# A longer list of steps at two seams of a two-layer trunk, its loads held back, and an attention mask written by VectorE

## The chip, the core and the metric

The kernel runs on one core of one Trainium2 chip. The core has a TensorE (matrix products, PE in the profile, its weight loads apart as PEld), a VectorE (DVE), a ScalarE (ACT), a GpSimd (POOL, all but unused here) and a SyncE (SP), whose queue issues most of the loads. The engines run side by side and wait for each other on semaphores. The metric is the device time of one execution in microseconds, the median of several runs.

## The reference

A trunk of two layers over a sequence of 1024 rows of 1024 columns, in float32:

```
for l in (0, 1):
    h = modulate(rmsnorm(x, norm_g[l, 0]), sh_m, sc_m)
    if l == 0: y = short_conv_mixer(h, ...)              # 1024 -> 3072, gated conv, -> 1024
    else:
        k_nope, v, k_pe = shared_kv(x, ...)              # latent keys and values of 8 heads
        y = mla_mixer(h, ..., k_nope, v, k_pe, ...)      # attention, blocks of 128 queries
    x = x + g_m * rmsnorm(y, norm_g[l, 1])
    h = modulate(rmsnorm(x, norm_g[l, 2]), sh_f, sc_f)
    y = square(relu(h @ w_up)) @ w_down                  # 1024 -> 4096 -> 1024
    x = x + g_f * rmsnorm(y, norm_g[l, 3])
```

In the attention a block of 128 queries sees the keys up to its own end, and a mask in chunks of 64 applies:

```
s = q_nope . k_nope + q_pe . k_pe
mask = (k // 64) <= (q // 64)
s = where(mask, s, finfo(float32).min);  p = softmax(s);  o = p @ v
```

Within the last 128 columns of a block's scores it is one quadrant that the mask blanks: the first 64 queries against the last 64 keys.

## The kernel before

**Products.** A float32 factor is kept as two parts: a rounded high part, written by a ScalarE copy (L176), and the low rest, written by a VectorE subtraction (L177). A product is three matmuls (`mm`, L173): low by high, high by low, high by high. Most of TensorE's work has this form and this line.

**The up projections.** `w_up` has 32 blocks of 128 columns, taken as 16 pairs. After a first, pre-split part, a pair is computed by a scheme with seven half-size products (Strassen's kind): sums of the pair's four quarters are formed by VectorE (`pair_sums`, L529, L530, L534, L537) and split into t2, s2 and t3; the products 5, 4 (from t2), 6 (from s2), 7 and 3 (from t3) follow, and VectorE adds them up (the takes at L583, L594, L603, L609). Loads of a pair are `load_pair`; the raw weights go into a ring of four buffers, or, for each third pair, into two buffers of their own (`up`, tag `raw`).

**The seams.** Ahead of each of the two MLPs, the stage before ends in rows of the residual stream: eight steps of norms and sums, each row then transposed (`tr0_0` and so on, L421), scaled by ScalarE (`tu`, L425) and split by VectorE into the moving factors (`b0`, L432, L433), and quarters summed (`D1` to `D9`, `P1` to `P5`, L445, L455, L458). `first_pairs` mixes this with the first up products: `fi` and `se` are the first and second products of the first five blocks, `ev1` and `ev2` their evictions, `spa` and `spd` the splits of the fourth and fifth block's weights (each loaded by `late` into one buffer `w`), `S1`, `t2a`, `t2d`, `S2`, `s2a`, `S3`, `s2d`, `t3a`, `t3d` the sums and splits of the first pair (a: high part by ScalarE, d: low part by VectorE) and `p3_0` to `p7_3` the products of the first pair, each in four parts. The order of these steps stands in the list `ORDER`. While the list runs, `pinned` fixes that order on every engine but SyncE. The scheduler of the framework orders the rest by its own priorities. When the list is done, six VectorE sums add up the first pair (L737 to L742), and the second pair is loaded, summed and split by `all_pairs`, as the later ones are. The two seams lie at about 374 to 441 us and 1512 to 1580 us.

**SyncE's queue.** Loads are issued in the queue's order; a load whose buffer isn't free holds up those behind it. The loads of the fourth block's weight and of the first pair are written outside `pinned`; the scheduler has put them in the midst of the stage before (the output product of the first layer's mixer, whose factors are the loads `raw<-hd` and conv_out_w).

**The attention.** `scores` computes a block of 128 queries of one head against n keys into PSUM (`big`) with five matmuls for each 512 columns (L1437), then a further matmul adds the mask: `mask_l` is 1 in the first 64 columns of one row, `mask_r` is -2^127, and the product lands on the last 64 columns (L1438). VectorE takes the negative maximum of each row (L1440), ScalarE writes the exponential and its sum (L1443), VectorE scales by the reciprocal (L1447, L1448), and TensorE transposes the result (L1463) for the product with the values. There are 8 heads of 8 blocks: 64 such calls.

Of the kernel before, what the change touches and what calls it, by code (L numbers as in the profile page):

```python
# [8 lines left out]
F32 = mybir.dt.float32  # L9
F32R = mybir.dt.float32r  # L10
# [34 lines left out]
mm5 tr0_0 tr0_1 tu0_0 mm6 add5 b0_0 sq5 rc4 pre4 stt5 tu0_1 xad5 tr0_2 tr0_3 tu0_2 add6 mm7 sqx5 b0_2 sq6 b0_1 rc5  # L45
pre5 stt6 tu0_3 xad6 dma5 tr0_4 tr0_5 tu0_4 add7 sqx6 tr0_6 b0_3 tu0_6 mul7 fi0 tu0_5 rc6 sq7 b0_4 b0_5 pre6 tr0_7
fi1 stt7 ev1_0 tu0_7 b0_6 sqx7 b0_7 fi2 ev1_1 rc7 S1 dma7 pre7 dma6 tr1_0 ev1_2 se0 tu1_0 P1_0 D1_0 D3_0 P2_0 tr1_1
D2_0 ev2_0 spa3 se2 D6_0 D4_0 P3_0 spd3 P4_0 tu1_1 D5_0 fi3 D8_0 P5_0 D7_0 ev2_2 D9_0 P1_1 t2a D3_1 tr1_2 D1_1 ev1_3
se1 t2d P2_1 tu1_2 D6_1 S2 P1_2 D2_1 se3 s2a D3_2 spa4 D4_1 ev2_1 spd4 P3_1 P4_1 D7_1 fi4 ev2_3 s2d D5_1 D8_1 P5_1
S3 p4_0 D9_1 t3a p6_0 D1_2 tr1_3 t3d P2_2 p6_1 tu1_3 D2_2 p5_1 D6_2 p7_0 P3_2 D4_2 p3_0 P1_3 D7_2 ev1_4 p7_1 P4_2  # L50
D5_2 se4 D3_3 P5_2 D8_2 D9_2 D1_3 p4_2 ev2_4 D2_3 p3_2 P2_3 D4_3 P3_3 p5_2 D6_3 P4_3 p7_2 D5_3 p6_2 D8_3 P5_3 p5_0
D7_3 p3_1 D9_3 p4_1 p4_3 p5_3 p7_3 p3_3 p6_3
# [4 lines left out]
C_ID, C_ML, C_MR, C_T = 0, 128, 256, 320  # L57
C_COLS = 2368
# [3 lines left out]
def trunk_kernel(ctx: ExitStack, tc: tile.TileContext, x, c, ada_w, ada_b, norm_g, conv_in_w, conv_w,  # L62
# [104 lines left out]

    mask_l = cp.tile([P, P], F32R, name="mask_l")
    mask_r = cp.tile([P, CHUNK], F32R, name="mask_r")
# [380 lines left out]
    def all_pairs(up, ops, jobs):  # L550
# [6 lines left out]
        for raws, begun, quarter, done, between in jobs:  # L557
            ra, rb = raws()
# [3 lines left out]
            if begun is None:  # L562
                w = up_split(up, ra)
# [10 lines left out]
            for part in pair_sums(up, ra, rb):  # L574
                rest.update(part or {})
# [70 lines left out]
    def first_pairs(seam, acts, up, wmat, ws, ops):  # L646
# [48 lines left out]
        late(3)  # L695
        a, b = load_pair(wmat, 0, up)
        a11, a12, a21, a22 = a[:, 0:4, :], a[:, 4:8, :], b[:, 0:4, :], b[:, 4:8, :]
        sums = {}
# [4 lines left out]
        def begin():  # L703
# [3 lines left out]
        def s2():  # L707
            sums["s2"] = high(a21, tuple(up.tile([P, 4, P], F32R, tag="s2" + "hl"[i], name=nm("s2"), bufs=1) for i in range(2)))

        acts["S1"] = begin  # L710
        acts["t2a"] = lambda: sums.update(t2=high(b))
        acts["t2d"] = lambda: low(sums["t2"], b)
        acts["S2"] = lambda: diff(a21, a22, a11)
        acts["s2a"] = s2
        acts["S3"] = lambda: diff(a12, a12, a21)
        acts["s2d"] = lambda: low(sums["s2"], a21)
        acts["t3a"] = lambda: sums.update(t3=high(a))
        acts["t3d"] = lambda: low(sums["t3"], a)

        def piece(j, kk):  # L720
# [4 lines left out]
            w = sums[w]  # L725
# [5 lines left out]

        with pinned():
            for name in ORDER:
                acts[name]()
            p1, cb = ca[0][:, HALF:], row_tile()
            c21, c22 = halves(cb)
            nc.vector.tensor_tensor(c21, p1, out_[6], op=ALU.add)  # L737
            nc.vector.tensor_tensor(c22, c21, out_[5], op=ALU.add)
            nc.vector.tensor_tensor(c21, c21, out_[4], op=ALU.add)
            nc.vector.tensor_tensor(p1, c22, out_[3], op=ALU.add)  # L740
            nc.vector.tensor_tensor(c22, c22, out_[7], op=ALU.add)
# [902 lines left out]
```

## Time and profile before

| what | value |
|---|---|
| median of 3 runs | 2173.43 us (2172.13 to 2174.46) |
| the profiled execution | 2171.63 us |
| its span, first to last instruction | 2169.8 us |
| its mean granted TensorE clock | 0.992 |
| busy: TensorE, VectorE, ScalarE | 2098.7, 1524.6, 1061.4 us |
| list of steps of the first seam | 372 to 436 us |
| list of steps of the second seam | ends at 1575.7 us |
| scores and products of the attention | 1135 to 1430 us |

A row of a timeline shows the start and the duration in us, the engine, the line, the operation, out<-in, the form and the count; in brackets what the engine waited for just before, and for how long. Names are those of the program without their numbers: `one`, `mm`, `tp` and `big` are PSUM banks, `slot` and `ring` are split factors, `uphi` and `uplo` are the high and low parts of t2 or t3 (or of a block's weight), `s` is s2 (its two parts, numbers and suffixes left out), `q` and `sums` the sums of quarters, `y` rows of results. VectorE and ScalarE rows are longer than their spacing by some 0.1 us, since an instruction starts before the one ahead has written its end.

### The profile page before, as it was taken

The numbers are of one execution on the slowest core, as the hardware profiler recorded it, in microseconds if no ns is written. First come the engines' busy times: TensorE is split into PE (matmuls) and PEld (weight loads), VectorE is DVE, ScalarE is ACT, GpSimd is POOL, SyncE is SP. The second block draws the span as 40 slices with busy tenths as digits, with TensorE's granted clock in tenths as the row PEclk, the third lists the DMA queues.
The fourth block names the chain that finished last, engine by engine and source line by source line (L and its number), as shares of the span: only waits on it lengthen the run. The fifth ranks groups of instructions, "written<-read, shape, count | busy, mean of one in ns | idle before, by whom it ended". The sixth has DMA issues, their size and how long they took to land.

```text
span 2169.8 us, 25308 instructions
## 1 busy us (share of the span) xinstructions
PE 2098.7 (97%) x9702; PEld 1729.0 (80%) x9702; DVE 1524.6 (70%) x2001; ACT 1061.4 (49%) x1512; POOL 4.0 (0%) x8
## 2 busy tenths in 40 slices
PE   6999999999999999999899999999999999999998
PEld 5888878778888778888777888877778887788887
DVE  5877766977665578956788776665976665558556
ACT  4533354845444434344665555564844544444342
POOL 0000000000000000000000000000000000000000
PEclk9999999999999999999999999999999999999999
DMA  8344464356543976445224231053355553853243
GB/s 244 103 148 132 145 219 140 89 187 204 167 150 112 328 267 243 167 144 175 78 61 120 76 113 45 25 175 131 89 184 174 174 176 112 305 194 127 97 146 136
DMA packets 242335, 330.95 MB, mean 153 GB/s; under 512 B 18629, under 2 KB 143906, under 8 KB 242214
## 3 DMA queue, kind: packets, MB, share of 16 engines
q1 hardware_dynamic: 204328, 248.57, 36.2%
q10 hardware_dynamic: 37886, 80.77, 9.8%
q8 instruction: 76, 1.25, 0.2%
q14 instruction: 45, 0.37, 0.0%
HBM read 248.55 MB, written 80.74 MB: 152 GB/s over the span
## 4 chain that ended last, share of the span: by engine, by line
PE 72%; DVE 13%; ACT 7%; DMA 6%; issue 2%; ACTq 0%; SPq 0%; DVEq 0%
PE one L173 36%; PE mm L173 18%; PE tp L173 7%; PE big L173 5%; DMA raw<-in_ada_w_dram 3%; PE big L1437 2%; ACT junk L258 2%; DVE y L318 1%; DVE raw L319 1%; DVE acc L198 1%; PE tp L1463 1%; DMA raw<-in_mlp_up_w_dram 1%; DVE y L312 1%; DMA raw<-ha 1%; DVE small L1440 1%
## 5 line engine op out<-in xcount | busy, mean ns | idle before, releaser
L173 PE MATMUL one<-slot,uphi 128*128 128x512 f32 x1240 | 382.1, 390 | 0.0
L173 PEld LDWEIGHTS one<-slot,uphi 128*128 128x128 f32 x1240 | 232.8, 188 | 48.7 <-issue 0.5
L173 PE MATMUL big<-slot 128*128 128x512 f32 x1152 | 266.9, 392 | 2.4 <-ACT y L887 1.9
L173 PEld LDWEIGHTS big<-slot 128*128 128x128 f32 x1152 | 216.2, 188 | 47.9 <-ACT y L887 2.4
L173 PE MATMUL one<-slot,uplo 128*128 128x512 f32 x620 | 242.8, 392 | 2.1 <-ACT y L581 2.1
L173 PE MATMUL one<-ring,ring 128*128 128x512 f32 x1008 | 232.4, 391 | 6.9 <-DVE ring L177 6.9
L176 ACT ACTIVATE ring<-w 128x1024 fp32r<-128x1024 f32 x98 | 103.7, 1058 | 261.5 <-PE tp L173 131.2
L173 PEld LDWEIGHTS one<-ring,ring 128*128 128x128 f32 x1008 | 188.2, 188 | 49.9 <-DVE ring L177 5.7
L177 DVE TENSOR_TENSOR uplo<-raw,uphi 128x1024 fp32r<-128x1024 f32 x121 | 147.7, 1223 | 78.0 <-ACT uphi L176 78.0
L177 DVE TENSOR_TENSOR ring<-w,ring 128x1024 fp32r<-128x1024 f32 x98 | 119.8, 1223 | 110.4 <-ACT ring L176 110.4
L176 ACT ACTIVATE uphi<-raw 128x1024 fp32r<-128x1024 f32 x121 | 128.0, 1059 | 136.8 <-PE one L173 82.4
L173 PE MATMUL mm<-ring,ring 128*128 128x512 f32 x672 | 162.5, 390 | 0.0
L173 PE MATMUL tp<-ring,ring 128*128 128x512 f32 x672 | 161.8, 389 | 0.0
L173 PE MATMUL mm<-slot,uphi 128*128 128x512 f32 x504 | 159.1, 397 | 0.0
L173 PEld LDWEIGHTS mm<-ring,ring 128*128 128x128 f32 x672 | 125.7, 188 | 27.1 <-DVE ring L177 0.6
L173 PEld LDWEIGHTS tp<-ring,ring 128*128 128x128 f32 x672 | 126.2, 188 | 26.2
L198 DVE SCALAR_TENSOR_TENSOR acc<-raw,csil,acc 128x1024 f32<-128x1024 f32 x88 | 112.8, 1282 | 46.6 <-DMA raw<-in_ada_w_dram 43.7
L173 PEld LDWEIGHTS one<-slot,uplo 128*128 128x128 f32 x620 | 116.4, 188 | 27.8 <-ACT y L581 3.3
L177 DVE TENSOR_TENSOR ring<-raw,ring 128x1024 fp32r<-128x1024 f32 x98 | 119.5, 1220 | 18.1 <-ACT ring L176 18.1
L173 PE MATMUL one<-slot,s 128*128 128x512 f32 x468 | 117.4, 402 | 9.2 <-DVE s L177 9.2
L173 PEld LDWEIGHTS one<-slot,s 128*128 128x128 f32 x468 | 91.0, 195 | 29.4 <-DVE s L177 10.1
L173 PEld LDWEIGHTS mm<-slot,uphi 128*128 128x128 f32 x504 | 95.6, 190 | 20.4 <-issue 1.4
(278 smaller groups left out, 3449.5 us busy)
## 6 DMA issues: line engine op xcount, KB each, us to landing
ha<-y ACTq DMA_DIRECT2D x196, 256.0 KB, 2.9
raw<-ha SPq DMA_DIRECT2D x98, 512.0 KB, 4.3
raw<-in_ada_w_dram SPq DMA_DIRECT2D x80, 512.0 KB, 4.7
raw<-in_mlp_up_w_dram SPq DMA_DIRECT2D x70, 512.0 KB, 5.1
w<-in_mlp_down_w_dram SPq DMA_DIRECT2D x56, 512.0 KB, 4.9
raw<-hd SPq DMA_DIRECT2D x24, 512.0 KB, 4.9
xs<-raw ACTq DMA_DIRECT2D x24, 512.0 KB, 2.8
raw<-xs SPq DMA_DIRECT2D x24, 512.0 KB, 3.8
```

What stands on the lines that cost most here:

```text
L173: nc.tensor.matmul(out_, lhs[a], rhs[b], start=first and i == 0, stop=last and i == 2, skip_group_check=more)
L176: nc.scalar.activation(hi, src, AF.Copy)
L177: nc.vector.tensor_tensor(lo, src, hi.bitcast(F32), op=ALU.subtract)
L198: nc.vector.scalar_tensor_tensor(acc, raw, s, acc, op0=ALU.mult, op1=ALU.add)
L258: nc.scalar.activation(junk, src, AF.Square, accum_out=ss)
L312: nc.vector.tensor_tensor(y, y, p_, op=ALU.add)
L318: nc.vector.scalar_tensor_tensor(y, y, rroot(ss), self.gmb, op0=ALU.mult, op1=ALU.mult)
L319: nc.vector.tensor_tensor(xr, xr, y, op=ALU.add)
L1437: nc.tensor.matmul(o_, a, m_, start=j == 0, stop=j == 4 and b * HALF + w < n)
L1440: nc.vector.tensor_reduce(mx, sp[:, :n], AX.X, ALU.max, negate=True)
L1463: nc.tensor.transpose(p_[:, c:c + P], pts[4 * hf + i][:, j * P:(j + 1) * P], ident)
```

## The change

Three things change.

**The list.** `ORDER` goes on through the second pair: `nS1`, `nt2a`, `nt2d`, `nS2`, `ns2a`, `nS3`, `ns2d`, `nt3a`, `nt3d` are its sums and splits, and `o6`, `o5`, `o4`, `o3`, `o7` are the six sums of the first pair, which stood behind the list. All steps have another order. `all_pairs` takes the second pair as it comes out of the list (`ready`).

**The loads.** The loads of the second pair (now in the two buffers of `up`, i % 3 == 1), of the fourth block's weight and of the first pair are written, in this order, under `pinned` for SyncE alone, so each stands behind the one before it, and behind the last load of x.

**The mask.** The mask matmul and its factors go (with 192 columns of the constants' input; the first load of constants has 128 columns instead of 320). VectorE writes -2^127 into the 64 by 64 quadrant of PSUM before the maximum.

SyncE around the first seam: `w` is the fourth (then the fifth) block's weight, names with in_mlp_up_w are weights of the up projection, those with hd and conv_out_w factors of the stage before, those with in_x rows of x. Before:

```order
L127 DMA raw_397_2470<-in_conv_out_w_dram 128x1024
L127 DMA w_478_2881<-in_mlp_up_w_dram 128x8x128
L127 DMA raw_398_2474<-hd2_118 128x1024
L127 DMA raw_399_2478<-in_conv_out_w_dram 128x1024
L127 DMA raw_400_2482<-hd3_119 128x1024
L127 DMA raw_479_2883<-in_mlp_up_w_dram 128x8x128
L127 DMA raw_480_2885<-in_mlp_up_w_dram 128x8x128
L127 DMA raw_409_2598<-in_conv_out_w_dram 128x1024
L127 DMA raw_410_2602<-hd4_120 128x1024
```

And after, further on in the same queue:

```order
L127 DMA raw_477_2875<-in_x_dram 128x1024
L127 DMA raw_478_2877<-in_mlp_up_w_dram 128x8x128
L127 DMA raw_479_2879<-in_mlp_up_w_dram 128x8x128
L127 DMA w_480_2881<-in_mlp_up_w_dram 128x8x128
L127 DMA raw_481_2883<-in_mlp_up_w_dram 128x8x128
L127 DMA raw_482_2885<-in_mlp_up_w_dram 128x8x128
L127 DMA w_533_3169<-in_mlp_up_w_dram 128x8x128
```

The weight (478, now 480), the first pair (479 and 480, now 481 and 482) moved behind the last load of x (477), with the second pair (478 and 479) ahead of them.

VectorE at the end of the first seam's list. Before, `q_563` is D9_3, 565 and 566 are the second pair's raw blocks, 569 and 573 the low parts of its t2 and t3, 571 that of its s2, 576 and 577 the third pair's blocks:

```order
L458 TENSOR_TENSOR q_563_3409<-sums_562_3383,q_563_3409 128x512
L177 TENSOR_TENSOR uplo_569_3458<-raw_566_3452,uphi_568_3457 128x1024
L530 TENSOR_TENSOR raw_588_3608<-raw_588_3608 128x512
L534 TENSOR_TENSOR raw_566_3452<-raw_566_3452,raw_565_3450 128x512
L537 TENSOR_TENSOR raw_565_3450<-raw_565_3450,raw_566_3452 128x512
L529 TENSOR_TENSOR raw_576_3512<-raw_576_3512,raw_577_3514 128x512
L737 TENSOR_TENSOR y_564_3437<-y_519_3104,mm_552_3317 128x512
L177 TENSOR_TENSOR uplo_573_3468<-raw_565_3450,uphi_572_3467 128x1024
L738 TENSOR_TENSOR y_564_3437<-y_564_3437,mm_557_3342 128x512
L177 TENSOR_TENSOR s2_571_3463<-raw_566_3452,s2_570_3462 128x512
```

After, with the second pair in 478 and 479, its low parts 555 (t2), 572 (t3) and 569 (s2):

```order
L681 TENSOR_TENSOR uplo_555_3326<-raw_479_2879,uphi_554_3325 128x1024
L455 TENSOR_TENSOR q_567_3415<-sums_564_3380,q_567_3415 128x512
L702 TENSOR_TENSOR raw_479_2879<-raw_479_2879,raw_478_2877 128x512
L526 TENSOR_TENSOR raw_576_3508<-raw_576_3508,raw_577_3510 128x512
L702 TENSOR_TENSOR raw_478_2877<-raw_478_2877,raw_479_2879 128x512
L757 TENSOR_TENSOR y_570_3439<-y_531_3151,mm_563_3370 128x512
L681 TENSOR_TENSOR s2_569_3437<-raw_479_2879,s2_568_3436 128x512
L681 TENSOR_TENSOR uplo_572_3445<-raw_478_2877,uphi_571_3444 128x1024
L757 TENSOR_TENSOR y_570_3439<-y_570_3439,mm_556_3328 128x512
```

The low part of s2 now stands ahead of that of t3 and of the sum with product 5, and the fourth pair's sums (raw_587, raw_588) have left the list.

TensorE at the border of the second and third pair. Before, `one_567` is the second pair's running bank, `one_578` the third pair's; slot_368 with s2 is product 6, slot_371 product 5, slot_370 product 3:

```order
L173 MATMUL one_567_3454<-slot_371_2322,uplo_569_3458 128x512
L173 MATMUL one_567_3454<-slot_371_2322,uphi_568_3457 128x512 x2
L173 MATMUL one_578_3516<-slot_368_2319,s2_582_3525 128x512
L173 MATMUL one_578_3516<-slot_368_2319,s2_581_3524 128x512 x2
L173 MATMUL one_578_3516<-slot_368_2319,s2_582_3525 128x512
```

After (the second pair's bank is `one_573`):

```order
L170 MATMUL one_573_3466<-slot_371_2318,uplo_555_3326 128x512
L170 MATMUL one_573_3466<-slot_371_2318,uphi_554_3325 128x512 x2
L170 MATMUL one_573_3466<-slot_370_2317,uplo_572_3445 128x512
L170 MATMUL one_573_3466<-slot_370_2317,uphi_571_3444 128x512 x2
L170 MATMUL one_578_3512<-slot_368_2315,s2_582_3521 128x512
```

The first three matmuls of the second pair's product 3 moved ahead of the third pair's product 6. On VectorE the take of the bank before them (L583) and the low part of the third pair's s2 have changed places: before the split stood first, now the take does.

The diff, without most of the list's rows:

```diff
-mm5 tr0_0 tr0_1 tu0_0 mm6 add5 b0_0 sq5 rc4 pre4 stt5 tu0_1 xad5 tr0_2 tr0_3 tu0_2 add6 mm7 sqx5 b0_2 sq6 b0_1 rc5
...
-D7_3 p3_1 D9_3 p4_1 p4_3 p5_3 p7_3 p3_3 p6_3
+mm5 tr0_0 tr0_1 add5 tu0_0 mm6 b0_0 sq5 rc4 tu0_1 stt5 pre4 b0_1 tr0_2 tr0_3 add6 tu0_2 mm7 tu0_3 xad5 sq6 b0_3 sqx5
+stt6 dma5 rc5 xad6 pre5 tr0_4 add7 tr0_5 sqx6 b0_2 tu0_4 rc6 sq7 fi1 mul7 b0_4 tu0_5 dma6 stt7 pre6 tr0_6 tr0_7 fi2
+tu0_6 b0_5 sqx7 b0_6 tu0_7 rc7 fi0 pre7 b0_7 ev1_2 nS1 ev1_1 spa3 S1 tr1_0 ev1_0 se2 tu1_0 spd3 P1_0 D1_0 dma7 D3_0
...
+P5_3 p6_0 nt2d p4_1 p3_2 D9_3 nS2 p6_3 nS3 p7_3 ns2a o6 p4_3 nt3a ns2d p5_3 nt3d o5 o4 p3_3 o3 o7
@@ load_pair
-            raw = up.tile([P, D], F32, tag="raw", name=nm("raw"), bufs=2) if up and i % 3 == 0 else raw_tile()
+            raw = up.tile([P, D], F32, tag="raw", name=nm("raw"), bufs=2) if up and i % 3 == 1 else raw_tile()
@@ all_pairs
-            for part in pair_sums(up, ra, rb):
-                rest.update(part or {})
+            if isinstance(ready, dict):
+                rest = ready
+            else:
+                for part in pair_sums(up, *ready):
+                    rest.update(part or {})
@@ first_pairs
-        late(3)
-        a, b = load_pair(wmat, 0, up)
+        with pinned([mybir.EngineType.SP]):
+            pair1 = load_pair(wmat, 1, up)
+            late(3)
+            pairs = [load_pair(wmat, 0, up), pair1]
...
+        for i, name in enumerate(("", "n")):
+            acts[name + "S1"] = lambda i=i: begin(i)
+            acts[name + "t2a"] = lambda i=i: sums[i].update(t2=high(pairs[i][1]))
+            acts[name + "t2d"] = lambda i=i: low(sums[i]["t2"], pairs[i][1])
...
+        acts["o6"] = lambda: plus(c2(0), p1(), 6)
+        acts["o5"] = lambda: plus(c2(1), c2(0), 5)
+        acts["o4"] = lambda: plus(c2(0), c2(0), 4)
+        acts["o3"] = lambda: plus(p1(), c2(1), 3)
+        acts["o7"] = ends
...
-        return [ca[i] for i in range(AHEAD)], cb
+        return [ca[i] for i in range(AHEAD)], ca["b"], ready
@@ mlp_up
-        end = all_pairs(up, ops, [(lambda i=i: load_pair(mlp_up_w[l], i, up), ca[i] if i < AHEAD else None, quarter,
+        end = all_pairs(up, ops, [(lambda i=i: ready if i == 1 else load_pair(mlp_up_w[l], i, up), ca[i] if i < AHEAD else None, quarter,
@@ scores
-                nc.tensor.matmul(o_, a, m_, start=j == 0, stop=j == 4 and b * HALF + w < n)
-        nc.tensor.matmul(sp[:, n - CHUNK:n], mask_l, mask_r, start=False, stop=True)
+                nc.tensor.matmul(o_, a, m_, start=j == 0, stop=j == 4)
+        nc.vector.memset(sp[:CHUNK, n - CHUNK:n], MASKED)
```

More of the change, by code (lines that the diff above doesn't have):

```diff
@@ L704, in begin @@
+        def begin(i):
+            a11, a12, a21, a22 = quarters(i)
             diff(a11, a11, a21)
             diff(a21, a21, a22, ALU.add)
[L707 to L718, printed above, removed]
+        def s2_sum(i):
+            a11, a12, a21, a22 = quarters(i)
+            diff(a21, a22, a11)
+        def s2_high(i):
+            part_ = tuple(up.tile([P, 4, P], F32R, tag="s2" + "hl"[j], name=nm("s2"), bufs=1) for j in range(2))
+            sums[i]["s2"] = high(quarters(i)[2], part_)
```

65 lines of the change are left out of this document (36 added, 29 removed).

## The prediction

> **What bounds the kernel now.** I read the page first (busy time, then the chain that ended last), then busy time by stretch, then TensorE's timeline at the places the change touches, then what VectorE, ScalarE and SyncE do just before.
>
> ```profile
> span 2169.8 us, 25308 instructions
> ...
> PE 2098.7 (97%) x9702; PEld 1729.0 (80%) x9702; DVE 1524.6 (70%) x2001; ACT 1061.4 (49%) x1512; POOL 4.0 (0%) x8
> ...
> PE 72%; DVE 13%; ACT 7%; DMA 6%; issue 2%; ACTq 0%; SPq 0%; DVEq 0%
> ...
> raw<-in_mlp_up_w_dram SPq DMA_DIRECT2D x70, 512.0 KB, 5.1
> ```
>
> TensorE is busy 97% of the span, so a change is worth what it takes out of TensorE's idle 71 us, or out of its own work, or what it puts in. By stretch (busy us of TensorE, weight loads, VectorE, ScalarE, GpSimd, then granted clock, DMA share and GB/s):
>
> ```profile
> core 0: us, PE busy (x) PEld busy (x) DVE busy (x) ACT busy (x) POOL busy (x), PEclk, DMA share, GB/s
> 372.00:436.00 64.00, 61.88 (x301) 50.67 (x300) 57.12 (x88) 50.10 (x84) 0.95 (x1) 1.00 0.35 106
> ...
> 1135.00:1430.00 295.00, 284.07 (x1614) 240.16 (x1612) 224.04 (x399) 165.05 (x328) 0.00 (x0) 0.99 0.23 75
> ```
>
> The first row is the list of steps of the first seam: TensorE idles 2.1 of 64 us, VectorE 6.9. The second is the attention with the masks: TensorE idles 10.9 us. What the seams cost stands behind their lists:
>
> ```profile
> 435.81 0.84 PE L173 MATMUL mm<-slot,s 128*128 128x512 f32 x3
> ...
> 440.77 4.39 PE L173 MATMUL one<-slot,s 128*128 128x512 f32 x12 [4.12 <-DVE s L177]
> ...
> 450.44 2.88 PE L173 MATMUL one<-slot,s 128*128 128x512 f32 x12
> ...
> 1579.88 4.61 PE L173 MATMUL one<-slot,s 128*128 128x512 f32 x12 [4.20 <-DVE s L177]
> ...
> 1589.80 2.88 PE L173 MATMUL one<-slot,s 128*128 128x512 f32 x12
> ```
>
> The list's last product ends at 436.65; TensorE then has nothing for 4.12 us (4.20 in the second seam), until VectorE has written the low part of the second pair's s2 (the last row of part 1's first fence). The twelve matmuls behind the wait take 4.39 and 4.61 us, where the same twelve of the third pair take 2.88: 1.51 and 1.73 us more, at a lower clock. So each seam pays 5.6 to 5.9 us.
>
> **Part 1, the longer list.** What VectorE does in that wait:
>
> ```profile
> 426.41 0.69 DVE L529 TENSOR_TENSOR raw<-raw,raw 128x512 f32<-128x512 f32 x1 [0.55 <-DMA raw<-in_mlp_up_w_dram]
> ...
> 433.04 1.22 DVE L177 TENSOR_TENSOR uplo<-raw,uphi 128x1024 fp32r<-128x1024 f32 x1
> ...
> 437.09 0.69 DVE L529 TENSOR_TENSOR raw<-raw,raw 128x512 f32<-128x512 f32 x1 [0.90 <-DMA raw<-in_mlp_up_w_dram]
> ...
> 438.30 1.22 DVE L177 TENSOR_TENSOR uplo<-raw,uphi 128x1024 fp32r<-128x1024 f32 x1
> 439.43 0.68 DVE L738 TENSOR_TENSOR y<-y,mm 128x512 f32<-128x512 f32 x1
> 440.03 0.68 DVE L177 TENSOR_TENSOR s<-raw,s 128x512 fp32r<-128x512 f32 x1
> ```
>
> The low part of s2 ends at 440.71. The new list gives VectorE the same sums and splits before it, except four that now stand behind it: the low part of t3 (pitch 439.43 - 438.30 = 1.13), the sum with product 5 (0.60) and the two sums of the fourth pair (0.60 each): 2.93 us. The two waits for loads, 0.55 and 0.90 us, go too if the second pair's loads stand ahead of the first's, as they now do. 440.71 - 2.93 - 1.45 = 436.33. The list's TensorE work is the same set of matmuls, so its end stays at 436.65, less the 0.34 of the row below, hence 436.3. The two meet: TensorE's wait is 0 to 0.3, and I take 0.05, with the slow clock gone too. The nearest bounds are 0 and the whole old wait (4.12), the latter if VectorE falls 4 us behind inside the list. What hides the moved 4.1 us of VectorE's work (six sums and low parts of the second pair) is its 6.9 idle us in the first row above.
>
> ```profile
> 433.18 0.73 PE L173 MATMUL one<-q,uphi 128*128 128x512 f32 x2 [0.34 <-DVE q L458]
> ```
>
> First seam: -4.1 - 1.5 - 0.3; second: -4.2 - 1.7 - 0.3.
>
> At the front of the list the order changes too:
>
> ```profile
> 382.49 0.66 PE L421 MATMUL tp<-cs,y 128*128 128x128 f32 x4 [0.73 <-ACT q L425]
> ...
> 389.93 0.66 PE L421 MATMUL tp<-cs,y 128*128 128x128 f32 x4 [0.43 <-ACT q L425]
> ...
> 389.35 1.21 DVE L334 TENSOR_TENSOR y<-y,big 128x1024 f32<-128x1024 f32 x1
> ...
> 390.94 0.69 DVE L433 TENSOR_TENSOR slot<-q,slot 128x512 fp32r<-128x512 f32 x1
> ```
>
> The waits of the transposes, 0.73 and 0.43, have other work in front of them now and go. But b0_2 stands behind add7 (389.35) now, and fi1, which needs it, comes next on TensorE. If add7 keeps its time, the low part is there at 391.6 (390.94 + 0.69); TensorE comes at some 390.3 (389.93 less the 0.43, and with the transposes that the new order still has ahead, of some 0.1 us each): 1.3 us lost against 1.2 won. I take nothing; ends -1 and +1.5.
>
> **Part 2, the seam of pairs 1 and 2.** With the second pair ready early, the scheduler puts the first three matmuls of its product 3 ahead of the third pair's product 6. They add to the bank that VectorE's take (L583) still has to read:
>
> ```profile
> 450.64 0.69 DVE L583 TENSOR_TENSOR y<-y,one 128x512 f32<-128x512 f32 x1 [0.60 <-PE one L173]
> ```
>
> Now TensorE goes on at 450.44 with a fresh bank, beside that take. After the change its next matmul must let the take finish (451.33, and that row waited for TensorE, so it can't come sooner): 0.9 us, at most 0.7 more where the third pair's s2 low part, now queued behind the take, comes late. I take +0.95 in each seam. Does such a wait slow the clock as well?
>
> ```profile
> 279.41 4.63 PE L173 MATMUL one<-slot,s 128*128 128x512 f32 x12 [0.87 <-DVE s L177]
> ```
>
> Here a wait of 0.87 us stands ahead of twelve matmuls that take 4.63 us, so it may: +1.5 each is a rival. The Trainium skill ("TensorE: Matmul & The Clock Gate", section "What's actually happening") says the clock halves only after an idle window of about 3.4 us, whose start runs free. The rows at 440.77 and 1579.88 agree with that, the row at 279.41 does not; by the rule the new wait would cost its 0.95 and no clock.
>
> Net: -4.95 and -5.25, together -10.2.
>
> **Part 3, the loads held back.** The three loads of a seam (0.5 MB each) leave the midst of the stage before and go behind the last load of x. There they had delayed one load that TensorE needed:
>
> ```profile
> 295.50 1.47 SPq L127 DMA_DIRECT2D raw<-in_mlp_up_w_dram  x2
> ...
> 300.21 6.49 DMA raw<-hd
> 306.72 1.06 ACT L176 ACTIVATE slot<-raw 128x1024 fp32r<-128x1024 f32 x1 [0.23 <-DMA raw<-hd]
> ...
> 308.74 5.51 PE L173 MATMUL big<-slot 128*128 128x512 f32 x23 [1.94 <-ACT y L887]
> ```
>
> Without the two loads at 295.50 the one at 300.21 is issued up to 1.47 us sooner, and lands quicker than 6.49. ScalarE's next step waited for it only 0.23, so part of its lateness is ScalarE's own queue: bounds 0 and -1.9; I take -1.0. At the other place (around 1433) TensorE waits for nothing of the kind: 0. What is held back must still come in time. The first pair's loads need buffers that come free behind the x rows of pre5 and dma5; from the place of these in the new list I put their issue at about 390.4, an estimate, and at 5.1 us they land about 396. The pair's first sum stands just ahead of tr1_0, the transpose at 399.79 below: 4 us of slack. The weight of the fifth block was issued at 406.19; it goes out behind spd3, which stands some 4 us earlier in the new list.
>
> ```profile
> 399.79 0.76 PE L421 MATMUL tp<-cs,y 128*128 128x128 f32 x5 [0.18 <-ACT y L362]
> ...
> 406.19 0.38 SPq L127 DMA_DIRECT2D w<-in_mlp_up_w_dram  x1
> ```
>
> So 0 here; if a load comes 4 us late, the list stops for those 4 us.
>
> **Part 4, the mask.** 64 matmuls and their weight loads go, and 64 VectorE writes of 64x64 come, between the last score matmul and the maximum:
>
> ```profile
> L1438 PE MATMUL big<-mask_r,mask_l 128*128 128x64 f32 x64 | 13.3, 207 | 0.0
> ...
> L1438 PEld LDWEIGHTS big<-mask_r,mask_l 128*128 128x128 f32 x64 | 12.3, 192 | 0.7
> ...
> L1440 DVE TENSOR_REDUCE small<-big 128x1 f32<-128x128 f32 x8 | 2.2, 281 | 0.0
> ...
> L1447 DVE RECIPROCAL small<-small 128x1 f32<-128x1 f32 x64 | 10.2, 160 | 18.8 <-ACT p L1443 18.8
> ...
> PE big L1437 <- ACT p L1443: 3.6, 8, 1.4
> ...
> 1241.29 0.19 PE L1438 MATMUL big<-mask_r,mask_l 128*128 128x64 f32 x1
> 1241.32 0.63 PE L1463 MATMUL tp<-cs,p 128*128 128x128 f32 x4
> ```
>
> The 207 ns are mostly the pipeline: the next matmul starts 0.03 us behind the mask's. Each frees 0.03 us at least, and 0.19 at most: 64 of them 2 to 12; near the lower end, at 0.07, 4.5. No row shows the write; it lies between the reciprocal of one column (0.160) and the maximum over 128 columns of PSUM (0.281): say 0.2 us, 64 x 0.2 = 13 us of VectorE, which idles 71 of these 295 us. It lengthens the way from scores to exponential by 0.2 less the mask matmul's 0.19, plus what the maximum loses in waiting for a write of its own engine, 0 to 0.2. TensorE waits 8 times for the exponential, 3.6 us in all; I add 2.5. Net -2, ends -6 and +6. The Trainium skill (same page, "LDWEIGHTS (loading the stationary operand)") gives a weight load one column per 1/1.2 ns, which would be 6.8 us for the 64, as an estimate; the row at 1241.32 shows most of it hidden.
>
> The constants lose 96 KB of their first load; at the 512 KB in 5.1 us of the page's row that is under 1 us, if anything waits for it: -0.3 (0 to -1).
>
> **Sum.** -10.2 - 1.0 - 2.0 - 0.3 = -13.5 against the profiled execution's 2171.63: 2158.1. That execution is 1.80 below the median of the runs (2173.43), so 2160 on their scale.
>
> **The rivals.**
> - The wait moves into the list: a load or VectorE is late by about as much as before (the fifth block's weight, b0_2, the first pair's sums). For it: VectorE is busy 57 of 64 us there. Against: its idle time is larger than the work added. Half of both waits stay and the clock drops: +4 to +6, 2164 to 2166; with all of it, +11, 2171, no change to be measured.
> - The new wait at pairs 1 and 2 halves the clock: +3, 2163.
> - Slower than before: the masks' write lies on TensorE's way. Its place is between the last score matmul and L1440. To cross 2177.8 (0.2% over 2173.43, or 4.35 us, about what a measurement can tell) attention must cost 2178 - 2160 + 2 = 20 us more, 0.3 us for each of 64; the write and its engine's own wait give at most 0.4, and only if every row of TensorE's score work waits for it, against the 8 that do now.
> - The masks do nothing and the held loads do nothing: +3, 2163.
>
> **Chances.** The forecast, with the clock case and the idle masks: 2154 to 2165, 0.57. Better (masks' upper bound, the whole of the load's 1.9): 0.08. The wait moves in part, 2165 to 2169: 0.15; in whole, 2169 to 2175: 0.11. Slower, by the masks or by a new list that waits more than the old: 0.09. Faster 0.80, same 0.11, slower 0.09. The range reaches from 2150 to 2173, which leaves out some 14 in 100 above it and 3 below; the forecast's own is 2154 to 2165.
>
> **What would show it.** Right: TensorE's first twelve matmuls behind the list take 2.9 us with no wait ahead; a 0.9 us wait for L583 at the start of the third pair; attention's stretch 0 to 6 us shorter, its waits for L1443 somewhat longer; the 308.74 wait gone or shorter. Wrong: waits of several us for VectorE or a load inside the list, or attention longer than 295 us.

## The result

The changed kernel takes 2151.42 us (median of 4 runs, 2150.18 to 2154.07) against 2172.78 us (4 runs, 2170.39 to 2174.46) of the kernel before: a ratio of 0.9904, with a 95% interval from 0.9887 to 0.9921. That is 21 us, or 1.0%, faster; forecast were 13.5 us, in a range from 2150 to 2173 that holds the time. It lies below the 2154 to 2165 that had a chance of 0.57, in the better case that had 0.08.

The page of the changed kernel (span, busy time, the chain that ended last):

```profile
span 2149.3 us, 25252 instructions
...
PE 2083.8 (97%) x9638; PEld 1712.5 (80%) x9638; DVE 1530.3 (71%) x2063; ACT 1060.0 (49%) x1512; POOL 4.0 (0%) x8
...
PE 73%; DVE 12%; ACT 7%; DMA 5%; issue 2%; SPq 0%; ACTq 0%; DVEq 0%
```

TensorE is as full as before, 97% of a span that is 20.5 us shorter. Its work lost 14.9 us (masks, and matmuls at the full clock that ran slower before), its idle time 5.6 us: what went at the lists' ends was in part spent elsewhere.

TensorE's timeline at the end of the two lists and at the border of the second and third pair:

```profile
432.28 2.88 PE L170 MATMUL one<-slot,s 128*128 128x512 f32 x12
...
441.38 0.50 PE L170 MATMUL one<-slot,uplo 128*128 128x512 f32 x1 [0.78 <-DVE y L583]
441.72 0.63 PE L170 MATMUL one<-slot,uphi 128*128 128x512 f32 x2
442.19 2.92 PE L170 MATMUL one<-slot,s 128*128 128x512 f32 x12
...
1560.05 2.88 PE L170 MATMUL one<-slot,s 128*128 128x512 f32 x12
...
1569.15 0.50 PE L170 MATMUL one<-slot,uplo 128*128 128x512 f32 x1 [0.78 <-DVE y L583]
```

The first row is the second pair's product 6: no wait ahead of it, where 4.12 us stood, and twelve matmuls in 2.88 us instead of 4.39; the row at 1560.05 is the same in the second seam (4.20 us and 4.61 before). The wait of 0.78 for the take (L583) is new, in both seams; the twelve matmuls behind it run at the full clock.

VectorE there (the row with `s` is the low part of s2, the one TensorE waits for):

```profile
428.89 0.70 DVE L526 TENSOR_TENSOR raw<-raw,raw 128x512 f32<-128x512 f32 x1
429.49 0.70 DVE L702 TENSOR_TENSOR raw<-raw,raw 128x512 f32<-128x512 f32 x1
430.09 0.70 DVE L757 TENSOR_TENSOR y<-y,mm 128x512 f32<-128x512 f32 x1
430.69 0.70 DVE L681 TENSOR_TENSOR s<-raw,s 128x512 fp32r<-128x512 f32 x1
431.38 1.23 DVE L681 TENSOR_TENSOR uplo<-raw,uphi 128x1024 fp32r<-128x1024 f32 x1
```

It ends at 431.39, 0.9 us ahead of the matmul that needs it, and the sum of the third pair (428.89) doesn't wait for its load any more. At the front of the list and in the stage before:

```profile
304.75 4.49 PE L170 MATMUL big<-slot 128*128 128x512 f32 x19
...
387.36 0.50 PE L170 MATMUL mm<-slot,uplo 128*128 128x512 f32 x1 [0.89 <-DVE slot L429]
388.08 0.74 PE L170 MATMUL mm<-slot,uphi 128*128 128x512 f32 x2 [0.22 <-DVE slot L430]
```

The wait of 1.94 us for the factor loaded late is gone from the first row; the second and third are fi1's wait for b0_2.

One way to see where the time went is to take the matmuls that both kernels issue and subtract the start in the trace before from the start in the trace after:

| place (us in the trace before) | shift, us | what happened since the row above |
|---|---|---|
| 81 | +0.6 | start |
| 283.87 | -1.2 | twelve matmuls behind 279.41 at the full clock |
| 308.74 | -3.3 | the wait for the late load |
| 382.49 | -4.3 | the wait of the transposes |
| 440.77 | -8.5 | the wait at the end of the first list |
| 443.86 | -10.0 | the slow clock behind it |
| 453.84 | -8.9 | the new wait at the border |
| 1127.64 | -9.4 | several small differences of both signs |
| 1433.54 | -15.4 | the attention; the trace before has two slow stretches of the clock there, the trace after none |
| 1471.14 | -14.6 | |
| 1521.32 | -15.5 | the wait of the transposes |
| 1579.88 | -19.8 | the wait at the end of the second list |
| 1585.95 | -21.6 | the slow clock behind it |
| 1593.20 | -20.5 | the new wait at the border; unchanged to the end |

Two rows were not forecast in this size: the loads, and the attention with 6.0 us.

### The profile page after: what moved, and what is told of

Its sections match the earlier page's. It is cut to its first block, busy times and chain, and to the rows that moved or that the text cites. A ratio compares the mean times of both kernels' runs of the same rounds, so it can differ in the third digit from the quotient of the medians.

```text
span 2149.3 us, 25252 instructions
## 1 busy us (share of the span) xinstructions
PE 2083.8 (97%) x9638; PEld 1712.5 (80%) x9638; DVE 1530.3 (71%) x2063; ACT 1060.0 (49%) x1512; POOL 4.0 (0%) x8
## 4 chain that ended last, share of the span: by engine, by line
PE 73%; DVE 12%; ACT 7%; DMA 5%; issue 2%; SPq 0%; ACTq 0%; DVEq 0%
PE one L170 38%; PE mm L170 19%; PE tp L170 6%; PE big L170 4%; ACT junk L255 2%; DMA raw<-in_ada_w_dram 2%; PE big L1465 2%; DVE y L315 1%; DVE raw L316 1%; DVE acc L195 1%; PE tp L1491 1%; DMA raw<-in_kv_ada_w_dram 1%; DVE ring L174 1%; ACT small L257 1%; DVE y L309 1%
## 5 line engine op out<-in xcount | busy, mean ns | idle before, releaser
L174 DVE TENSOR_TENSOR uplo<-raw,uphi 128x1024 fp32r<-128x1024 f32 x117 | 142.8, 1223 | 79.0 <-ACT uphi L173 78.9
L173 ACT ACTIVATE uphi<-raw 128x1024 fp32r<-128x1024 f32 x117 | 123.7, 1059 | 135.6 <-PE one L170 76.9
L170 PE MATMUL one<-slot,s 128*128 128x512 f32 x468 | 112.6, 389 | 0.6 <-DVE s L174 0.6
L581 ACT ACTIVATE y<-one 128x512 f32<-128x512 f32 x62 | 36.7, 592 | 142.8 <-PE one L170 98.5
```

The lines of the kernel that those rows point to most:

```text
L170: nc.tensor.matmul(out_, lhs[a], rhs[b], start=first and i == 0, stop=last and i == 2, skip_group_check=more)
L173: nc.scalar.activation(hi, src, AF.Copy)
L174: nc.vector.tensor_tensor(lo, src, hi.bitcast(F32), op=ALU.subtract)
L581: nc.scalar.activation(dst, x_, AF.Copy)
```

## The experiments

Ratios are to the kernel before on the same chip, with their 95% intervals. The kernel before run again as if it were a new one gave 0.9989 [0.9979, 0.9999]; so 0.1% can't be told from nothing here, and for smaller effects the traces decide.

### The parts by themselves

**The mask alone, and no mask at all.** In the first kernel the list and the loads are as before and VectorE writes the mask; in the second, nothing blanks the quadrants, so the masking is left out.

```diff
-                nc.tensor.matmul(o_, a, m_, start=j == 0, stop=j == 4 and b * HALF + w < n)
-        nc.tensor.matmul(sp[:, n - CHUNK:n], mask_l, mask_r, start=False, stop=True)
+                nc.tensor.matmul(o_, a, m_, start=j == 0, stop=j == 4)
+        nc.vector.memset(sp[:CHUNK, n - CHUNK:n], MASKED)      # the first kernel alone
```

> The kernel before with the mask alone written by VectorE (list and loads as before). Ledger theory: the 64 matmuls free 4.4 us of TensorE, its waits in the attention grow by 2.6, so 1.8 us faster, some 2171. Rival: the mask is worth what the whole attention stretch lost between the two traces (about 5 us, the rest being a TensorE clock that drops less there), so some 2167 to 2168. If the write stands on TensorE's way: 2173 or more.

> The kernel before without any mask: neither the 64 matmuls nor a write, so the blanked quadrants stay in the softmax. If a mask matmul costs only its own spacing (0.07 us), 4.4 us faster, a ratio of 0.998; then the kernel with the mask written by VectorE, 5.4 us faster, would beat one without a mask, which it can't. If it costs its neighbours too (in the attention's middle, 41 of them went and TensorE's spacing shrank by 5.5 us with no less idle time, 0.13 us each), some 8 us, a ratio of 0.9963, and VectorE's write then costs the difference to 5.4.

Measured: 2168.27 us, 0.9975 [0.9966, 0.9984], or 5.4 us faster (3.5 to 7.4), with the mask by VectorE; 2166.52 us, 0.9967 [0.9954, 0.9979], or 7.2 us faster (4.6 to 10.0), without any. So a mask matmul costs 0.11 us (7.2 / 64) by the median and 0.07 to 0.16 by the interval, with its own spacing of 0.07 at the lower end; the two intervals overlap, so what the write costs (1.8 us by the medians) can't be told from nothing. The traces narrow it down. The attention between two matmuls that both kernels issue, before and with the mask by VectorE (the columns as in the prediction's table by stretch):

```profile
1127.64:1433.54 305.90, 294.89 (x1655) 248.79 (x1654) 233.86 (x410) 171.70 (x338) 0.95 (x1) 0.99 0.23 75
```

```profile
1131.68:1432.50 300.82, 288.41 (x1592) 239.08 (x1591) 240.19 (x474) 170.90 (x338) 0.96 (x1) 0.99 0.24 75
```

5.1 us less, at the same mean clock: TensorE is busy 6.5 us less and idle 1.4 us more. The 64 mask matmuls had 4.5 us of spacing of their own, so up to 2 us lie elsewhere: some neighbours come closer (transposes at 96 ns before and 93 after, the products of 256 columns with v at 213 and 184), others less close (the scores of 384 columns at 176 and 199), and 0.5 us is the clock at the end. Whether the mask's weight load held them up these rows don't show. And the write is cheap; VectorE's groups of the changed kernel:

```profile
L1466 DVE MEMSET big<- 64x64 f32 x64 | 7.2, 112 | 7.0 <-PE big L1465 6.0
...
L1468 DVE TENSOR_REDUCE small<-big 128x1 f32<-128x128 f32 x8 | 2.3, 286 | 0.1
```

0.112 us each, and VectorE idles 0.7 us in all ahead of the 64 maxima behind it.

**All but the mask.** The changed kernel with the mask matmul put back (the diff above, the other way round, with its constants).

> The changed kernel with the mask matmul put back. Ledger theory: 1.8 us slower than the changed kernel, some 2153, and the two slow-clock stretches of the trace before that lie outside the seams (at 279.41 and near 1430) may or may not be there, since nothing of this change touches them. Rival (the mask is worth 5 us): some 2156 to 2157.

Measured: 2157.91 us, 0.9925 [0.9913, 0.9938]. The mask's part is 0.9904 / 0.9925, again 0.2%, some 5 us. The two intervals overlap, so this alone would not show it; that the ledger's 1.8 us are too few rests on the 3.5 to 7.4 us of the first kernel. The traces of this kernel and the changed one have the same list and loads, and no slow clock in the attention:

```profile
1127.74:1433.56 305.82, 291.58 (x1665) 246.91 (x1664) 227.47 (x404) 169.90 (x335) 0.00 (x0) 1.00 0.25 78
```

```profile
1126.73:1426.65 299.92, 286.58 (x1601) 238.12 (x1599) 233.87 (x468) 168.62 (x335) 0.00 (x0) 1.00 0.25 79
```

5.9 us less: TensorE is busy 5.0 us less and idle 0.9 less. So the traces give 5.0 to 6.5 us of busy time for the 64 masks, 0.08 to 0.10 us each, a little over their own spacing; and the waits, which the ledger let grow by 2.6 us, changed by +1.4 and -0.9. The slow clock behind 279.41 is back in this trace (twelve matmuls in 4.61 us), so it was not the change that took it away.

**The loads alone, in both kernels.** In the kernel before, the two lines that load the fourth block's weight and the first pair are pinned; in the changed kernel the pinning is taken away (from the second pair's loads too).

```diff
+        with pinned([mybir.EngineType.SP]):
+            late(3)
+            a, b = load_pair(wmat, 0, up)
-        late(3)
-        a, b = load_pair(wmat, 0, up)
```

```diff
-        with pinned([mybir.EngineType.SP]):
-            pair1 = load_pair(wmat, 1, up)
-            late(3)
-            pairs = [load_pair(wmat, 0, up), pair1]
+        pair1 = load_pair(wmat, 1, up)
+        late(3)
+        pairs = [load_pair(wmat, 0, up), pair1]
```

> The kernel before with the fourth block's weight and the first pair's loads held behind the last load of x, nothing else. If these loads delay the one that TensorE needs at 308 us, its wait there (1.9 us in one trace, with a slow clock of 1.6 behind it in another) goes: 2 to 3.5 us faster, some 2170.5; the waits behind the lists stay. Rival (the loads then come late for the list): no gain, or slower.

> The changed kernel with the three loads (fourth block's weight, second pair) left to the scheduler, which issues them again in the midst of the stage before. If these loads delay the one that TensorE needs at 308 us, a wait of about 1.9 us is back there and the kernel is 2 to 2.5 us slower, some 2153.5. Rival (the gain at 308 has another cause, as the other order of the list): no wait, 2151.4.

Measured: the first 2169.42 us, 0.9979 [0.9970, 0.9989], so 4.5 us faster; its trace has no wait at 308 and keeps 4.18 and 4.20 us behind the lists, as expected. The second 2155.33 us, 0.9909 [0.9893, 0.9924], which by its ratio can't be told from the changed kernel; but its trace has the wait again:

```profile
310.91 5.32 PE L170 MATMUL big<-slot 128*128 128x512 f32 x15 [2.72 <-ACT y L916]
```

2.72 us, and fifteen matmuls in 5.32 us where nineteen take 4.49: 1.7 us of slow clock behind it. The kernel before, in its second trace, shows the same pair (2.41 us, 1.6 slow), where the first trace had 1.94 and the full clock. So these loads cost 2 to 4.4 us in these traces, by how long the wait is and whether the clock falls.

### What takes the wait at the end of the list away

**The second pair out of the list.** The changed kernel, all steps in their new order, but those of the second pair left to the general code.

```diff
-P5_3 p6_0 nt2d p4_1 p3_2 D9_3 nS2 p6_3 nS3 p7_3 ns2a o6 p4_3 nt3a ns2d p5_3 nt3d o5 o4 p3_3 o3 o7
+P5_3 p6_0 p4_1 p3_2 D9_3 p6_3 p7_3 p4_3 p5_3 p3_3 o6 o5 o4 o3 o7
...
-            pair1 = load_pair(wmat, 1, up)
             late(3)
-            pairs = [load_pair(wmat, 0, up), pair1]
+            pairs = [load_pair(wmat, 0, up)]
```

> The changed kernel with the second pair's steps taken out of the list and loaded, summed and split by the general code again; the six sums of the first pair stand at the list's end; all other steps in the new order. Prediction's theory (the longer list takes the wait away): waits of 3 to 4 us and the slow clock are back in both seams, 8 to 11 us slower than the changed kernel, some 2160 to 2163. Rival (the other order of the list and the later loads leave VectorE early enough by themselves, and the scheduler fits the second pair in): at most 2 us slower.

Measured: 2153.2 us, 0.9909 [0.9895, 0.9923]. The prediction's theory that the longer list does it falls: without it there is no wait at the end of either list.

```profile
436.62 2.88 PE L170 MATMUL one<-slot,s 128*128 128x512 f32 x12
```

The scheduler, left free, put the second pair's sums and splits among the list's steps, almost where the longer list pins them. The second pair's loads, not pinned here, stand in the stage before again, and a wait of 1.09 us at 309.48 is there; that is part of what this kernel is slower than the changed one by.

**The old order with the new loads, and the new order with the old loads.** The first is the kernel above with the old order in its list (mask by VectorE, loads held back, the second pair in its own buffers and loaded early). The second is the kernel before with the new order in its list and nothing else.

```diff
-ORDER: the new order, without n*
+ORDER: the old order, then o6 o5 o4 o3 o7
```

> The kernel of pair2_out with the old order of the list: the mask by VectorE, the fourth block's weight and the first pair held back, the second pair in its own two buffers and so loaded early, but no step of the second pair in the list. If the early loads of the second pair are what takes TensorE's wait away (its sums no longer wait for memory and the scheduler fits them in among the list's steps), TensorE's wait behind the list is 0 to 0.7 us in both seams, with no slow clock: some 2154. Rival (the new order of the list is what does it): waits of 3 to 4 us and the slow clock, some 2162.

> The kernel before with the new order of the list alone (without the second pair's steps), its loads and its mask as before. Early-loads theory: the second pair's loads still come late, its s2 low part stands behind five of the first pair's sums, TensorE waits 2.5 to 4 us behind the list, with the slow clock: 2170 to 2174. Rival (order): no wait, some 2162.

Measured: 2164.18 us, 0.9958 [0.9942, 0.9974], and 2170.51 us, 0.9990 [0.9980, 1.0001]. Neither takes the wait away: 3.51 and 3.30 us in the two seams of the first, 2.80 in both of the second, with the slow clock behind all four. The early-loads theory was wrong on the first; on the second the waits and the late place of s2's low part came as it said, but the part of the loads in that is not shown (below). What VectorE does in the first:

```profile
433.58 1.22 DVE L174 TENSOR_TENSOR uplo<-raw,uphi 128x1024 fp32r<-128x1024 f32 x1
434.71 0.68 DVE L527 TENSOR_TENSOR raw<-raw 128x512 f32<-128x512 f32 x1
438.73 0.69 DVE L526 TENSOR_TENSOR raw<-raw,raw 128x512 f32<-128x512 f32 x1 [3.33 <-DMA raw<-in_mlp_up_w_dram]
439.34 0.68 DVE L756 TENSOR_TENSOR y<-y,mm 128x512 f32<-128x512 f32 x1
439.94 0.69 DVE L174 TENSOR_TENSOR s<-raw,s 128x512 fp32r<-128x512 f32 x1
```

The sum at 438.73 is the fourth pair's; it waits 3.33 us for its weights, and the low part of the second pair's s2 stands behind it. ScalarE's row for the high part shows a second cause:

```profile
437.20 0.63 ACT L173 ACTIVATE s<-raw 128x512 fp32r<-128x512 f32 x1 [0.66 <-PE mm L170]
```

It waits for the last piece of the first pair's product 6, since s2 has one buffer, and in the old order that piece (p6_3) is the list's last step. So the low part could not have ended before 438.5 (437.83 and 0.69), and TensorE would have waited 1.3 us even without the late load, which brings the other 2.2 of the 3.51. In the new order p6_3 has four pieces of other products behind it; the same row of the changed kernel stands 2.5 us ahead of the list's end (432.28):

```profile
429.76 0.63 ACT L677 ACTIVATE s<-raw 128x512 fp32r<-128x512 f32 x1 [3.06 <-PE mm L170]
```

In the second kernel s2's low part (440.86) stands behind four of the first pair's sums and 1.58 us of waiting for the list's product 6. No VectorE instruction from 395 to 442 us waits for a load there; the second pair's sums stand late in the queue, and that the scheduler put them there because of the later loads is likely, but not shown:

```profile
436.12 0.69 DVE L737 TENSOR_TENSOR y<-y,mm 128x512 f32<-128x512 f32 x1 [1.58 <-PE mm L173]
...
440.86 0.68 DVE L177 TENSOR_TENSOR s<-raw,s 128x512 fp32r<-128x512 f32 x1
```

So what decides is when that one subtraction can run, and three things set it here: its place in VectorE's queue (the next experiment), the buffer of s2, which the order of the list frees early or late, and any sum ahead of it that waits for its load. With the new loads and the new order together none is late, whether the list pins the second pair or the scheduler happens to choose its places.

**The subtraction moved back.** The changed kernel, `ns2d` behind o4 in the first seam and behind o7 in the second.

```diff
-... ns2a o6 p4_3 nt3a ns2d p5_3 nt3d o5 o4 p3_3 o3 o7
+... ns2a o6 p4_3 nt3a p5_3 nt3d o5 o4 ns2d p3_3 o3 o7      # first seam
+... ns2a o6 p4_3 nt3a p5_3 nt3d o5 o4 p3_3 o3 o7 ns2d      # second seam
```

> The changed kernel with the low part of the second pair's s2 moved back in the list: behind o4 in the first seam, behind o7 in the second. By VectorE's durations it is 3.5 and 5.9 us later, less the margin of 0.9: TensorE waits some 2.6 and 5 us. If the clock drops behind any wait (as the row at 279.41 suggested), both groups of twelve matmuls take 4.4 us or more, +10.6 in all, some 2162; if it takes a wait that fills an idle window of about 3.4 us, the first takes 2.9 and the second 4.4, +9.1, some 2160.5.

Measured: 2163.25 us, 0.9955 [0.9941, 0.9969]; the waits are 3.19 and 5.55 us.

```profile
438.31 4.46 PE L182 MATMUL one<-slot,s 128*128 128x512 f32 x12 [3.19 <-DVE s L694]
...
1573.44 5.13 PE L182 MATMUL one<-slot,s 128*128 128x512 f32 x12 [5.55 <-DVE s L694]
```

The subtraction's place alone, all else as in the changed kernel, brings 11 of the 21 us back. Both groups of twelve are slow (4.46 and 5.13 against 2.88). The waits came out 0.6 us longer than reckoned, so the first doesn't show what a wait of 2.6 would have done; but 3.19 us is less than the 3.4 that the expectation's second case asks for, and the clock fell all the same (more in the last section). The wait at the border is gone from both seams, since the third pair's s2 is in time when TensorE comes later.

### Past the change

**The border.** The changed kernel with the first sums of the fourth and later pairs held behind the third pair's s2 low part.

```diff
         begin_ = nc.vector.tensor_tensor(a11, a11, a21, op=ALU.subtract)
+        if turn_[0] not in (None, "next"):
+            tc.add_manual_dep(begin_.ins, turn_[0], NO_SYNC, reason="pinned")
```

> The changed kernel, with the fourth and later pairs' first sums held behind the third pair's s2 low part, after which the scheduler puts the third pair's product 6 ahead of the second pair's product 3. If the take at L583 is what TensorE waits for at the border of these pairs, the wait of 0.78 and the slow start behind it (1.1 and 0.9 us) go in both seams: 2149.4, a ratio to the kernel before of 0.9895. Rival (TensorE then waits for the third pair's s2 instead): no change.

Measured: 2151.44 us, 0.9897 [0.9883, 0.9911]. The two waits of 0.78 are gone: the third pair's product 6 stands ahead of the second pair's product 3 again and follows without a gap.

```profile
443.05 3.03 PE L170 MATMUL one<-slot,s 128*128 128x512 f32 x12
...
442.30 0.69 DVE L538 TENSOR_TENSOR s<-raw,s 128x512 fp32r<-128x512 f32 x1
443.24 0.69 DVE L591 TENSOR_TENSOR y<-y,one 128x512 f32<-128x512 f32 x1 [0.24 <-PE one L170]
```

The shifts against the changed kernel's trace are -0.9 and -1.0 us at the two borders, near what was expected; the time by ratio is 1.5 us lower, less than the measurement tells.

**The front.** The kernel of the border, with b0_2 ahead of add7.

```diff
-stt6 dma5 rc5 xad6 pre5 tr0_4 add7 tr0_5 sqx6 b0_2 tu0_4 rc6 sq7 fi1 ...
+stt6 dma5 rc5 xad6 pre5 tr0_4 b0_2 add7 tr0_5 sqx6 tu0_4 rc6 sq7 fi1 ...
```

> The kernel of border, with b0_2 put ahead of add7 in the list. If fi1's wait at the front of the list (0.89 and 0.22 us in each seam) hangs on add7 standing ahead of b0_2, it goes and nothing takes its place: 2 us faster than border, a ratio to the kernel before of 0.9888. Rival: add7, later by 1.1 us, makes the next row's transposes (tr0_6, tr0_7) late by as much: no change.

Measured: 2148.97 us, 0.9888 [0.9871, 0.9904], not to be told from the border's. The trace shows the rival: fi1's wait of 0.89 goes and another comes, in both seams.

```profile
392.07 0.66 PE L419 MATMUL tp<-cs,y 128*128 128x128 f32 x4 [1.44 <-ACT q L423]
```

**The kernel before, a second trace.**

> The kernel before, unchanged, for a second trace. Clock theory: the seams' waits and the slow clock behind them are there again at both places, each over 4 us and 1.4 us; the slow stretches elsewhere (1.7 us behind 279.41, 1.3 behind 1144, 1.2 behind 1430) move, grow or vanish, since they hang on when the clock's window falls. Rival: all of them stand at the same places, so they belong to the kernel, and the change has removed them.

Measured: 2171.57 us, 0.9989 [0.9979, 0.9999]. The waits behind the lists are there again (4.09 and 4.32 us, 1.7 us of slow clock behind each). The slow stretch behind 279.41 is there (twelve matmuls in 4.51 us), so is that at 1144; that near 1430 is gone, and a new one of 1.6 us stands at 309. So neither side holds wholly: they keep to a few places, and whether and for how long the clock falls there changes from run to run.

## Why the prediction was right, and where its sizes were off

- **The ends of the lists** (part 1: -4.1 - 1.5 and -4.2 - 1.7): right. Between the traces the waits give 4.1 and 4.2 us and the clock 1.5 and 1.7. That VectorE's low part of s2 and the list's end would meet was right, with 0.9 us to spare where 0 was reckoned. The reason given, what VectorE has ahead of that subtraction and whether its loads are there, is what the runs show; that it needs the longer list is not. One row was misread: the load that VectorE waited 0.90 us for is the third pair's, not the second's; the wait went all the same. The order of the other steps with the early load of the second pair does it too, and each of these two alone does not. What the reckoning missed is s2's buffer: it asked only what VectorE has to do, and not that the old list's last step holds the buffer that the second pair's s2 needs.
- **The cover**: VectorE's idle time in the list (6.9 us) did take the added work. The rival of a wait that moves into the list is wrong as to place, but its mechanism is real: it is what the old order with the new loads shows, with a load of the fourth pair as the cause.
- **The front and D9_3** (0 and -0.3 in each seam): each list gained 1.0 us besides its end. fi1's wait came as reckoned (0.89 and 0.22 against 1.3 us), and what went outweighs it a little more. Of the same sign, within the ends given.
- **The border** (+0.95 in each): right, 1.1 us in each. That the new wait slows the clock, the rival, is wrong: 2.92 us for twelve.
- **The loads** (-1.0, ends 0 and -1.9): mis-sized. The wait went whole, 2.1 us between the two traces, and held alone the loads bring 4.5 us (2.4 to 6.5 by the interval). The step that failed was to take the late load's delay from one trace, as if 1.94 us without a slow clock were all it costs: five other traces with loads of the up projection in that place have waits of 2.4 to 3.0 us, and four of these 1.6 to 1.7 us of slow clock behind them. Two more, with the second pair's loads there, have 1.27 and 1.09; the six traces without such loads wait 0.3 us at most.
- **The mask** (-2, ends -6 and +6): the sign and the range right, the size not. Measured are -5.4. The step that failed is the sizes of its two terms: the matmuls were put at -4.5, from their own spacing of 0.07 us each, and TensorE's busy time in the attention fell by 6.5 and 5.0 in the two pairs of traces above; the waits were put at +2.5, and its idle time changed by +1.4 and -0.9. Between the traces before and after themselves the idle time did rise by 2.5, but the busy time fell by 8.5, with the two slow stretches of the clock gone as well. So the matmul term was too small by 0.5 to 2 us in the first two pairs, and that of the waits too large there by 1.1 and 3.4. The estimate that the prediction drew from the Trainium skill ("TensorE: Matmul & The Clock Gate", section "LDWEIGHTS (loading the stationary operand)") was 6.8 us for the 64 weight loads; the measured 7.2 (4.6 to 10.0) and the 5.0 to 6.5 of the traces tell neither that nor the prediction's 4.5 apart, so whether most of a load is hidden stays open. The write was put at 0.2 us, between two rows; it takes 0.112, less than both bounds.
- **The start** (-0.3): TensorE begins 0.6 us sooner and is 0.6 us later by 81 us. Nothing.
- Some 1.6 us of the difference between the two traces are the clock behind 279.41, which was slow in the trace before and in nearly all others, and was not in that of the changed kernel. It is no effect of the change that any run shows; the last section shows what it hangs on.
- Of the 7.9 us by which the gain exceeds the forecast, the loads and the mask account for 3.5 and 3.4 by the medians of their own runs, though both intervals are wide.

## What to carry to other kernels

When a fast engine waits for one instruction of a slower one, look at what stands ahead of that instruction in its queue, whether any of it waits for memory on behalf of work that is needed later, and what has to free its buffer; an order and the times of its loads have to be changed together, and either alone may show nothing. The price of a small matmul need not be its own spacing: compare a whole stage, with the same other matmuls, with and without it. A wait that slows the clock costs more than its idle time: here 1.0 to 2.6 us more in the matmuls behind it.

## What the runs showed of the hardware

How long a wait must be for TensorE's clock to fall behind it can be read over the fourteen traces. Behind a stream of 512-column matmuls, waits up to 1.94 us (dozens, among them 1.72 us at the second seam in most traces) were followed by the full clock; waits of 2.8 us and more behind such a stream cost 1.5 to 2.6 us more in the matmuls that follow; between them it changes from run to run with the same wait:

```profile
1078.48 0.66 PE L173 MATMUL mm<-slot,uplo 128*128 128x512 f32 x1 [2.02 <-ACT lat L1277]
```

```profile
1070.66 0.50 PE L170 MATMUL mm<-slot,uplo 128*128 128x512 f32 x1 [2.03 <-ACT lat L1305]
```

The first is of the kernel before, with a slow clock behind it, the second of the changed kernel, at the full clock, after the same wait. The granted clock settles why. In each of the fourteen traces it changes only at multiples of 3.41 us from each other (to a few ns), so a slow stretch of the kernel's middle lasts 3.41 or 6.83 us, and this grid lies elsewhere in each execution. The windows of 3.41 us on each trace's own grid, around the two waits (busy time of TensorE second, granted clock third from the end):

```profile
1075.25:1078.66 3.41, 1.39 (x7) 0.85 (x6) 3.41 (x6) 3.35 (x6) 0.00 (x0) 1.00 0.71 154
1078.66:1082.08 3.42, 3.42 (x11) 2.63 (x12) 1.70 (x3) 2.07 (x4) 0.00 (x0) 0.50 0.76 232
```

```profile
1066.52:1069.94 3.42, 2.11 (x10) 1.41 (x8) 3.42 (x7) 2.66 (x4) 0.00 (x0) 1.00 0.69 152
1069.94:1073.35 3.41, 2.69 (x16) 2.29 (x17) 2.64 (x4) 3.06 (x7) 0.00 (x0) 1.00 0.55 156
```

In the first the whole wait falls into one window, which is busy for 1.39 us, and the next window gets half the clock. In the second the wait is split over two windows, and the clock stays. Over all traces, without the first 60 and the last 20 us, take the windows at the full clock in which TensorE ran 512-column matmuls or nothing: the 28 that were busy for 1.43 us or less were all followed by half the clock, those busy for more than 1.75 us (some 6600) never were, and of the seven between five were and two were not. So it is not the length of the wait that decides, but whether one window is left with less than about half of its time in such matmuls.

Matmuls of one column count for little. A wait of 0.5 to 1.2 us did slow the clock where sixteen of them (1.84 us) stand ahead of it, as at 279.41, in all traces that have such a wait but that of the changed kernel. There the window from 276.53 holds 0.86 us of 512-column matmuls in the kernel before, and at most 1.30 in the other slow traces; in the changed kernel's trace the window from 278.04 holds 1.65. So the full clock there hangs on where the grid fell, which is luck, and not on the change.

The Trainium skill ("TensorE: Matmul & The Clock Gate", section "What's actually happening") has a free-running window of some 3.4 us. The grid of 3.41 us agrees with it; that it takes a whole idle window does not, since windows busy for up to 1.43 us, and some up to 1.74, were enough.
